# Transformer block on one core: FFN way down in blocks of twelve matmuls instead of triples, `h` moved by 64 bytes, and another order behind the last matmul

## The chip, the cores and the metric

One Trainium2 chip, one of its cores. The metric is the device time in microseconds of one execution of the whole program, all data in HBM at its start and its end.

## The reference

One block of a transformer on 512 tokens of width 1,024, all in float32: a gated FFN, a mixer of two kinds of attention, a second gated FFN, a last RMS norm. Cut to what matters here:

```python
def swiglu(h, w_gate, w_up, w_down):          # 1024 -> 2816 -> 1024
    return (jax.nn.silu(h @ w_gate) * (h @ w_up)) @ w_down

x = x + 0.5 * swiglu(rmsnorm(x, norm_ffn1), w_ffn1_gate, w_ffn1_up, w_ffn1_down)
x = x + hybrid_mixer(rmsnorm(x, norm_mix), ...)
x = x + 0.5 * swiglu(rmsnorm(x, norm_ffn2), w_ffn2_gate, w_ffn2_up, w_ffn2_down)
return rmsnorm(x, norm_final)
```

## The kernel before

Activations stand transposed: eight tiles `x` of 128 features by 512 tokens. Float32 products are made from halves: each operand is split into a rounded part and the rest (`whi`, `wlo` of down weights, `sph`, `spl` of gate and up weights, `h` twice for each hidden tile), and `mm3` (L100) issues three matmuls for one product: high by high, high by low, low by high. The kind of half is `fp32r`.

**The FFN** (class `Ffn`, L192). Hidden features come in 22 tiles `f` of 128, four to a group (`FP`). The first group is computed plainly (`plain`); the others in pairs by a seven-product scheme on blocks (`pair`), whose matmuls have 256 columns and write `pu`, `pv` and `pw`. For each of its steps ScalarE makes `sph`, VectorE `spl` from it, both in six buffers, four steps ahead of TensorE. The hidden tile `h` (tag `h`, pool `hp`) is kept as halves.

**The way down** (`down`, L392) multiplies a group's four hidden tiles with the down weights, for each of eight output tiles `d`: four products of 512 columns into one bank `pd`, so 12 matmuls, and VectorE adds half of the bank to `x` (`half_added`, L531). `mixed` lays the eight steps of one group between the pair steps of the next. In the kernel before, a step doesn't issue its matmuls itself: it puts four triples (`triple`, one `mm3` each) into a list `waiting`, and `run` of the pair steps takes one out with `between` after each of its own products of four, and a second in the middle when more than four wait. `issue_after` holds each triple behind the pair matmul ahead of it. So the 12 matmuls of a `d` stand in four places.

**The end** (from L1108 on). The last two hidden tiles are multiplied the other way round, `h` as weights and `w_down` as the streamed operand, so that the result has tokens on partitions. `turn_x` transposes `x` by TensorE (`px`, 32 of them) into eight tiles `z`. For each of four token tiles `i` and two halves of the width there are six matmuls into `pd`, `residual` adds them to `z` on VectorE (L1130) and sums squares on ScalarE (L1131), and `norm(i)` takes the root on ScalarE (L1135), the reciprocal on VectorE (L1136), scales one half on ScalarE (L1138) and the other on VectorE (L1139), and writes both by SyncE (L1141).

Tiles are placed by pools in the order in which they are asked for, so a tile that nothing reads moves those behind it: `gap` and `rest` are such. In the program before, halves of down weights and `h` both start at byte 32 modulo 256 of a partition; `sph` and `spl` start at byte 96, and what is streamed against them (`xo`, `th`, `tl`) at 32. A scheduler orders each engine's instructions on these dependences.

Of the kernel before, what the change touches and what calls it, by code (L numbers as in the profile page):

```python
# [9 lines left out]
F32 = mybir.dt.float32  # L10
F32R = mybir.dt.float32r
AF = mybir.ActivationFunctionType
# [17 lines left out]
def block_kernel(ctx: ExitStack, tc: tile.TileContext, A: dict, out: bass.AP):  # L30
# [69 lines left out]
    def mm3(p, w, v, first, last, again=False):  # L100
        nc.tensor.matmul(p, w[0], v[0], start=first, stop=False, skip_group_check=again)  # L101
        nc.tensor.matmul(p, w[0], v[1], start=False, stop=False, skip_group_check=again)  # L102
        return nc.tensor.matmul(p, w[1], v[0], start=False, stop=last, skip_group_check=again)  # L103

    def mm2(p, w, v, first, last):

# [21 lines left out]

    gates = cp.tile([128, NT, 24], F32, name="gates")
    pos = cp.tile([128, 2, 32], F32, name="pos")  # L130
    ss = cp.tile([128, 2, NT], F32, name="ss")
# [3 lines left out]
    cp.tile([128, 48], F32, name="rest")  # L135
# [56 lines left out]
    class Ffn:  # L192
# [14 lines left out]
        def __init__(self, wg, wu, which, tmp, hp, sp):  # L207
            self.w, self.which, self.tmp, self.hp, self.sp = (wg, wu), which, tmp, hp, sp
            self.xg, self.hs, self.steps = None, {}, []
            self.b, self.temps = {}, {}  # L210
            self.last_lo = None
            self.x_made = None
            self.waiting = []
            self.in_pair = None
            self.held = 5
# [91 lines left out]
        def pair(self, f):  # L307
# [36 lines left out]
            def copied(m, to, name):  # L344
                part[m, name] = self.sp.tile([128, HT], F32, name="wc", tag="wc", bufs=4)
# [43 lines left out]
                                  lambda m=m, then=then: then(m)])  # L389
            return steps  # L390

        def down(self, w, fs, then, tags=("mm",), groups=(1,) * NK, kept_back=True, left=None):  # L392


            n = len(fs)
            raw, got, bank = {}, {}, {}
# [14 lines left out]
            def run(d):  # L411
                ds = {sum(groups[:g]): range(sum(groups[:g]), sum(groups[:g + 1])) for g in range(len(groups))}.get(d)
                if ds is None:
                    return

                def triple(i, k):
                    if k == 0:
                        bank[i] = pt(tags[i % len(tags)], "pd")
                    with tc.issue_after(self.in_pair.ins) if left != 0 and self.in_pair else nullcontext():
                        mm3(bank[i], got[i, k], self.hs[fs[k]], k == 0, k == n - 1)  # L420
                    if k == n - 1:
                        then(i, bank[i])
# [4 lines left out]
                at = 0 if left is None else len(todo) - (left if ds[-1] == NK - 1 else 0)  # L427
                if at:
                    self.between(len(self.waiting))
                for one in todo[:at]:  # L430
                    one()
                self.waiting += todo[at:]
# [4 lines left out]
        def between(self, n):  # L437

            for _ in range(min(n, len(self.waiting))):
                self.waiting.pop(0)()  # L440

        def mixed(self, steps, fills, tail=1):

# [8 lines left out]
        def lay(self, wd):  # L452

            for f in range(FP):
                self.steps += self.plain(f)
            self.steps += self.down(wd[0], range(FP), half_added, ("s", "t", "o", "mm"), (4, 4), False, 1)
            fills = []
            for f in range(FP, NF, FP):
                fs = range(f, min(f + FP, NF))
                pairs = [step for i in fs[::2] for step in self.pair(i)]  # L460
                self.steps += self.mixed(pairs, fills) if fills else pairs
                if len(fs) == FP:
                    fills = self.down(wd[f // FP], fs, half_added)

        def go(self, after):
# [20 lines left out]
                late = s[4]  # L486
            if late:
                late()
            self.between(len(self.waiting))


    scr_t = dp.tile([16, 128, RVW], F32, name="scr_t")
# [40 lines left out]
    with ExitStack() as ph:  # L533
# [55 lines left out]
            squares(tmp, d, "tmp", 5)  # L589

        ffn.lay(A["wd1a"])
        ffn.steps += ffn.down(A["wd1b"], range(NF - NF % FP, NF), then, (None,), (4, 2, 2), left=0)
        ffn.go(after)


# [495 lines left out]
    with ExitStack() as ph:  # L1091
# [36 lines left out]
        def residual(i, half, p):  # L1128

            nc.vector.scalar_tensor_tensor(z[i, half], p, 0.5, z[i, half], ALU.mult, ALU.add)  # L1130
            nc.scalar.activation(sq, z[i, half], AF.Square, accum_out=ss[:, half, i:i + 1])  # L1131

        def norm(i):
            r = ss[:, 1, i:i + 1]
            nc.scalar.activation(r, r, AF.Sqrt, bias=mean[:, i:i + 1], scale=1.0 / D)  # L1135
            nc.vector.reciprocal(r, r)  # L1136
            y = [xp.tile([128, S], F32, name="xo", tag="xo", bufs=16) for _ in range(2)]
            nc.scalar.activation(y[0], z[i, 0], AF.Copy, scale=r)  # L1138
            nc.vector.scalar_tensor_tensor(y[1], z[i, 1], r, gf[1], ALU.mult, ALU.mult)  # L1139
            for half in range(2):  # L1140
                nc.sync.dma_start(out[i * 128:(i + 1) * 128, half * S:(half + 1) * S], y[half])  # L1141

        last = range(NF - NF % FP, NF)
        w = [load(A["wd2b"][half]) for half in range(2)]
# [2 lines left out]
                z[i, half] = turn_x(i, half)  # L1147
        for i in range(NT):
            b = slice(i * 128, (i + 1) * 128)
            for half in range(2):  # L1150
                p = pt(None, "pd")
                for k, f in enumerate(last):
                    mm3(p, (hs[f][0][:, b], hs[f][1][:, b]), w[half][k], f == last[0], f == last[-1])
                residual(i, half, p)
                if half == 0:
                    nc.gpsimd.tensor_scalar(mean[:, i:i + 1], ss[:, 0, i:i + 1], 1.0 / D, 1e-6, ALU.mult, ALU.add)
                    nc.gpsimd.tensor_tensor(z[i, 0], z[i, 0], gf[0], ALU.mult)
                else:
                    norm(i)


def _buckets(dist):
# [84 lines left out]
```

## Time and profile before

| what | value |
|---|---|
| three runs: median (lowest to highest) | 991.96 us (991.29 to 992.9) |
| the profiled execution | 990.21 us |
| its span, first to last instruction | 988.4 us |
| mean granted TensorE clock, of full speed | 0.997 |
| TensorE busy | 970.5 us, 98% of the span |
| VectorE, ScalarE, GpSimd busy | 778.5, 561.9, 132.5 us |
| first FFN, attention, second FFN with the end | to 351 us, 351 to 634 us, 634 us on |

The profiled execution took 1.8 us more than its span and 1.75 us less than the median. PE is the row of matmuls, PEld that of weight loads, which run beside them. A matmul's record is longer than the distance to the next one's start, since matmuls overlap; where two groups of one shape differ in mean length, their distances differ likewise.

### The profile page before, as it was taken

To read this page: it belongs to the slowest core of one execution; us is meant where nothing else is said; L and a number is where in the kernel's file an instruction comes from. 1 tells how busy PE (TensorE), PEld (TensorE's weight loads), DVE (VectorE), ACT (ScalarE), POOL (GpSimd) and SP (SyncE) were. 2 spreads that over 40 slices of the span, in tenths; PEclk is the share of its full clock that TensorE was granted. 3 is DMA by queue.
4 is the path that set the end of the run, shared out by engine and by line. 5 is a ranking of instruction groups with operands and counts; after the bars stand their busy time and mean duration, and the time that the engine had idled before them with its cause. 6 is when DMAs were issued, how large, how long until landed. Compare 5 with 4: busy or idle time off the path is not lost.

```text
span 988.4 us, 16902 instructions
## 1 busy us (share of the span) xinstructions
PE 970.5 (98%) x6084; PEld 859.0 (87%) x6084; DVE 778.5 (79%) x1579; ACT 561.9 (57%) x1165; POOL 132.5 (13%) x176
## 2 busy tenths in 40 slices
PE   9999999999999999999999999999999999999996
PEld 7789999999999898787878888888999999999985
DVE  6996997688776587768788978789898788777744
ACT  6464655445544366567677886655475445454435
POOL 0000000000000000035666676100000000000002
PEclk9999999999999999999999999999999999999998
DMA  7255534332321125531121232226254322341102
GB/s 257 97 185 173 196 129 133 110 102 91 97 68 43 58 88 190 181 113 33 53 72 43 87 85 80 71 86 213 67 166 153 119 73 95 101 128 44 54 11 86
DMA packets 50056, 104.52 MB, mean 106 GB/s; under 512 B 10129, under 2 KB 14690, under 8 KB 49972
## 3 DMA queue, kind: packets, MB, share of 16 engines
q1 hardware_dynamic: 49684, 102.91, 32.4%
q8 instruction: 48, 0.79, 0.3%
q10 hardware_dynamic: 288, 0.52, 0.1%
q14 instruction: 36, 0.29, 0.1%
HBM read 97.98 MB, written 5.30 MB: 104 GB/s over the span
## 4 chain that ended last, share of the span: by engine, by line
PE 91%; DVE 4%; issue 1%; ACT 1%; DMA 1%; POOL 0%; SPq 0%; POOLq 0%; ACTq 0%; DVEq 0%
PE pd L102 8%; PE pd L103 8%; PE pd L101 8%; PE pu L101 6%; PE pu L103 6%; PE pu L102 6%; PE pw L101 4%; PE pw L103 4%; PE pw L102 4%; PE pp L103 3%; PE pp L101 3%; PE pp L102 3%; PE pgu L102 3%; PE pgu L101 3%; PE pgu L103 3%; PE ps_t L940 3%
## 5 line engine op out<-in xcount | busy, mean ns | idle before, releaser
L236 ACT ACTIVATE sph<-aw 128x512 fp32r<-128x512 f32 x252 | 157.3, 630 | 197.4 <-PE pu L102 71.1
L237 DVE TENSOR_TENSOR spl<-aw,sph 128x512 fp32r<-128x512 f32 x252 | 172.3, 690 | 59.7 <-ACT sph L236 57.2
L92 ACT ACTIVATE whi<-raw 128x512 fp32r<-128x512 f32 (+1 forms) x200 | 121.5, 619 | 126.4 <-PE pd L102 44.2
L102 PE MATMUL pd<-h,whi 128*128 128x512 f32 x336 | 132.7, 395 | 0.0
L103 PE MATMUL pd<-h,wlo 128*128 128x512 f32 x336 | 131.1, 393 | 0.0
L96 DVE TENSOR_TENSOR wlo<-raw,whi 128x512 fp32r<-128x512 f32 (+1 forms) x168 | 111.7, 676 | 24.1 <-ACT whi L92 20.6
L101 PE MATMUL pd<-h,whi 128*128 128x512 f32 x336 | 130.4, 394 | 0.0
L101 PE MATMUL pu<-th,sph 128*128 128x256 f32 x432 | 119.4, 276 | 0.3 <-ACT wc L346 0.3
L103 PE MATMUL pu<-th,spl 128*128 128x256 f32 x432 | 119.4, 276 | 0.0
L102 PE MATMUL pu<-tl,sph 128*128 128x256 f32 x432 | 119.2, 276 | 0.0
L322 DVE TENSOR_TENSOR aw<-aw 128x512 f32<-128x512 f32 x144 | 99.0, 689 | 0.0
L531 DVE SCALAR_TENSOR_TENSOR x<-pd,x 128x512 f32<-128x512 f32 x88 | 60.1, 689 | 33.3 <-PE pd L103 33.3
L101 PEld LDWEIGHTS pu<-th,sph 128*128 128x128 f32 x432 | 81.1, 188 | 4.6 <-ACT wc L346 0.5
L102 PEld LDWEIGHTS pu<-tl,sph 128*128 128x128 f32 x432 | 81.1, 188 | 4.0
L103 PEld LDWEIGHTS pu<-th,spl 128*128 128x128 f32 x432 | 81.1, 188 | 0.1
L101 PE MATMUL pw<-xo,sph 128*128 128x256 f32 x288 | 79.7, 277 | 0.2 <-ACT sph L236 0.2
L102 PE MATMUL pw<-xo,sph 128*128 128x256 f32 x288 | 79.5, 276 | 0.0
L103 PE MATMUL pw<-xo,spl 128*128 128x256 f32 x288 | 79.4, 277 | 0.0
L103 PEld LDWEIGHTS pd<-h,wlo 128*128 128x128 f32 x336 | 63.1, 188 | 13.8
L102 PEld LDWEIGHTS pd<-h,whi 128*128 128x128 f32 x336 | 63.1, 188 | 4.0
L101 PEld LDWEIGHTS pd<-h,whi 128*128 128x128 f32 x336 | 63.1, 188 | 3.7
L101 PEld LDWEIGHTS pw<-xo,sph 128*128 128x128 f32 x288 | 54.1, 188 | 3.9 <-ACT sph L236 0.6
(246 smaller groups left out, 2443.1 us busy)
## 6 DMA issues: line engine op xcount, KB each, us to landing
aw<-in_wg SPq DMA_DIRECT2D x72, 256.0 KB, 2.8
aw<-in_wu SPq DMA_DIRECT2D x72, 256.0 KB, 4.5
raw<-in_wd1a SPq DMA_DIRECT2D x20, 512.0 KB, 3.9
raw<-in_wd2a SPq DMA_DIRECT2D x20, 512.0 KB, 4.8
raw<-in_w_a SPq DMA_DIRECT2D x16, 512.0 KB, 4.8
raw<-in_w SPq DMA_DIRECT2D x8, 512.0 KB, 4.0
raw<-in_w_o SPq DMA_DIRECT2D x8, 512.0 KB, 3.6
raw<-in_wg SPq DMA_DIRECT2D x7, 512.0 KB, 3.6
```

What stands on the lines that cost most here:

```text
L92: last_hi[0] = nc.scalar.activation(hi, v, AF.Copy)
L96: nc.vector.tensor_tensor(lo, v, f32(hi), ALU.subtract)
L101: nc.tensor.matmul(p, w[0], v[0], start=first, stop=False, skip_group_check=again)
L102: nc.tensor.matmul(p, w[0], v[1], start=False, stop=False, skip_group_check=again)
L103: return nc.tensor.matmul(p, w[1], v[0], start=False, stop=last, skip_group_check=again)
L236: nc.scalar.activation(hi, v, AF.Copy)
L237: self.last_lo = nc.vector.tensor_tensor(lo, v, f32(hi), ALU.subtract)
L322: nc.vector.tensor_tensor(to, x, y, op)
L531: nc.vector.scalar_tensor_tensor(xs[d], p, 0.5, xs[d], ALU.mult, ALU.add)
L940: nc.tensor.transpose(p[:, wide:wide + 128], lps[qi][:, j * 128:(j + 1) * 128], ident)
```

## The change

1. `down` loses the list of triples: a step issues its 12 matmuls at once. `between`, `waiting`, `in_pair` and `held` go.
2. Two tiles that nobody reads stand ahead of others: 64 bytes in `hp` ahead of `h`, and 192 bytes in `sp`. `h` starts at byte 96 modulo 256, so that weights' halves minus `h` is 192 where it was 0. All else stays in place modulo 256. With it, `sph` minus `h` (the first weights behind a run of `pd`) is 0 where it was 64, and in the last stage `h` as weights minus the streamed `w_down` is 64 where it was 0.
3. The last token tile's second half is computed in two pieces of 256 columns. `norm(i - 1)` is called behind tile `i`, its reciprocal behind the last addition to `z`, its `xo` behind a small addition; one of the last two output DMAs is issued by ScalarE.

```diff
+            hp.tile([128, 16], F32, name="gap_h", tag="gap_h", bufs=1)
+            sp.tile([128, 48], F32, name="gap_t", tag="gap_t", bufs=1)
...
-                    self.in_pair = mm3(bank[m, to], (hi[:, k], lo[:, k]), x, first and k == 0, k == 3, not first)
-                    if k == 1:
-                        self.between(self.held == 0 and len(self.waiting) > 4)
-                self.between(self.held == 0)
-                self.held = max(self.held - 1, 0)
+                    mm3(bank[m, to], (hi[:, k], lo[:, k]), x, first and k == 0, k == 3, not first)
...
-                todo = []
+                for i in ds:
+                    bank[i] = pt(tag, "pd")
                 for ks in ([range(n)] if len(ds) == 1 else [range(n - 1), range(n - 1, n)]):
-                    todo += [lambda i=i, k=k: triple(i, k) for i in ds for k in ks]
...
+                    for i in ds:
+                        for k in ks:
+                            mm3(bank[i], got[i, k], self.hs[fs[k]], k == 0, k == n - 1)
+                for i in ds:
+                    then(i, bank[i])
...
-        def norm(i):
-            r = ss[:, 1, i:i + 1]
+        def norm(i, part):
+            r = ss[:, part, i:i + 1]
             nc.scalar.activation(r, r, AF.Sqrt, bias=mean[:, i:i + 1], scale=1.0 / D)
-            nc.vector.reciprocal(r, r)
+            with tc.issue_after(added[0].ins):
+                nc.vector.reciprocal(r, r)
...
+                queue = nc.scalar if i == NT - 1 and half == 0 else nc.sync
+                queue.dma_start(out[i * 128:(i + 1) * 128, half * S:(half + 1) * S], y[half])
...
-            for half in range(2):
-                p = pt(None, "pd")
+            parts = [slice(0, S), slice(0, S)] if i < NT - 1 else [slice(0, S), slice(0, S // 2), slice(S // 2, S)]
+            for part, cols in enumerate(parts):
+                p = pt(None, "pd")[:, cols]
...
+                elif part < len(parts) - 1:
+                    summed_up[0] = nc.vector.scalar_tensor_tensor(
+                        mean[:, i:i + 1], ss[:, 1, i:i + 1], 1.0 / D, mean[:, i:i + 1], ALU.mult, ALU.add)
+            if i:
+                norm(i - 1, 1)
+        norm(NT - 1, 2)
```

What it does to the order. TensorE in the second FFN, before, at one triple (the numbers tell buffers apart):

```order
L103 MATMUL pu_10454<-xo_8272,spl_10385 128x256
L101 MATMUL pd_10434<-h_9673,whi_10337 128x512
L102 MATMUL pd_10434<-h_9674,whi_10337 128x512
L103 MATMUL pd_10434<-h_9673,wlo_10338 128x512
L102 MATMUL pv_10508<-xo_8255,sph_10414 128x256
```

and now, at one block:

```order
L103 MATMUL pu_10500<-th3_7814,spl_10558 128x256
L101 MATMUL pd_10674<-h_10035,whi_10582 128x512
L102 MATMUL pd_10674<-h_10036,whi_10582 128x512
L103 MATMUL pd_10674<-h_10035,wlo_10583 128x512
L101 MATMUL pd_10674<-h_10107,whi_10582 128x512
L102 MATMUL pd_10674<-h_10108,whi_10582 128x512
L103 MATMUL pd_10674<-h_10107,wlo_10583 128x512
L101 MATMUL pd_10674<-h_10413,whi_10582 128x512
L102 MATMUL pd_10674<-h_10414,whi_10582 128x512
L103 MATMUL pd_10674<-h_10413,wlo_10583 128x512
L101 MATMUL pd_10674<-h_10459,whi_10582 128x512
```

The block ends with two more and goes on with `pw`. Over the whole program before, 230 runs of `pd` have three matmuls; now 66 runs that follow on other matmuls have eight or more (51 of them twelve), and 17 have one to four. Both hold the same 1,008 matmuls on `h`. The order of attention is the same in both.

VectorE's last rows, before (`z` from `pd` is the addition of a half, `xo` an output):

```order
L1130 SCALAR_TENSOR_TENSOR z<-pd,z 128x512 x2
L1136 RECIPROCAL ss<-ss 128x1
L1130 SCALAR_TENSOR_TENSOR z<-pd,z 128x512
L1139 SCALAR_TENSOR_TENSOR xo<-z,ss,gf 128x512
L1136 RECIPROCAL ss<-ss 128x1
L1139 SCALAR_TENSOR_TENSOR xo<-z,ss,gf 128x512
```

and now:

```order
L1110 SCALAR_TENSOR_TENSOR z<-pd,z 128x512
L1110 SCALAR_TENSOR_TENSOR z<-pd,z 128x256 x2
L1117 RECIPROCAL ss<-ss 128x1
L1144 SCALAR_TENSOR_TENSOR mean<-ss,mean 128x1
L1121 SCALAR_TENSOR_TENSOR xo<-z,ss,gf 128x512
L1117 RECIPROCAL ss<-ss 128x1
L1121 SCALAR_TENSOR_TENSOR xo<-z,ss,gf 128x512
```

The third tile's reciprocal no longer stands ahead of the last addition, and that addition has 256 columns. ScalarE's last rows, before (`sqd` sums squares):

```order
L1131 ACTIVATE sqd,ss<-z 128x512
L1138 ACTIVATE xo<-z,ss 128x512
L1131 ACTIVATE sqd,ss<-z 128x512
L1135 ACTIVATE ss<-ss,mean 128x1
L1138 ACTIVATE xo<-z,ss 128x512
```

and now:

```order
L1111 ACTIVATE sqd,ss<-z 128x512
L1111 ACTIVATE sqd,ss<-z 128x256 x2
L1119 ACTIVATE xo<-z,ss 128x512
L1115 ACTIVATE ss<-ss,mean 128x1
L1119 ACTIVATE xo<-z,ss 128x512
L1124 DMA out<-xo 128x512
```

The third tile's `xo` has moved behind the last sum of squares and ahead of the last root. On TensorE the 32 transposes of `turn_x`, which before stood in five places between `pd` matmuls, now stand in one row ahead of the last stage.

## Rows read from the trace of the kernel before

**Rows 1.** The page, part 1 (busy time, share of the span, instructions of each engine) and part 4 (the chain that ended last, share of the span by engine).

```profile
PE 970.5 (98%) x6084; PEld 859.0 (87%) x6084; DVE 778.5 (79%) x1579; ACT 561.9 (57%) x1165; POOL 132.5 (13%) x176
...
PE 91%; DVE 4%; issue 1%; ACT 1%; DMA 1%; POOL 0%; SPq 0%; POOLq 0%; ACTq 0%; DVEq 0%
```

**Rows 2.** The windows view, the stretch of the second FFN in which its triples lie. Columns: stretch, its length, then busy us (and instructions) of PE, PEld, DVE, ACT, POOL, the granted clock, DMA share, GB/s.

```profile
710.00:940.00 230.00, 229.78 (x1692) 215.45 (x1691) 185.21 (x326) 120.49 (x236) 0.00 (x0) 1.00 0.33 106
```

**Rows 3.** The timeline, PE alone, around one triple: the last `pu` ahead of it, its first matmul, and the first matmul behind it. Columns: start us, us of the matmul, engine, line, operation, out<-in, tile, count.

```profile
251.13 0.28 PE L103 MATMUL pu<-th,spl 128*128 128x256 f32 x1
251.24 0.40 PE L101 MATMUL pd<-h,whi 128*128 128x512 f32 x1
...
251.94 0.28 PE L101 MATMUL pw<-xo,sph 128*128 128x256 f32 x1
```

**Rows 4.** The groups by line and form, PE alone, of the stretch 150 to 290 us, where every `pd` stands in a triple. Columns: busy us, mean ns of one, idle time before.

```profile
L102 PE MATMUL pd<-h,whi 128*128 128x512 f32 x73 | 29.0, 397 | 0.0
L101 PE MATMUL pd<-h,whi 128*128 128x512 f32 x73 | 28.8, 395 | 0.0
L103 PE MATMUL pd<-h,wlo 128*128 128x512 f32 x73 | 28.8, 394 | 0.0
```

**Rows 5.** The same view of the stretch 333.2 to 350.8 us, inside the one run of 84 `pd` matmuls at the end of the first FFN (the other two lines also have 389).

```profile
L102 PE MATMUL pd<-h,whi 128*128 128x512 f32 x26 | 10.1, 389 | 0.0
```

**Rows 6.** The timeline, PE alone: the 1st, the 7th and the 84th matmul of that run.

```profile
331.78 0.40 PE L101 MATMUL pd<-h,whi 128*128 128x512 f32 x1
...
333.16 0.39 PE L101 MATMUL pd<-h,whi 128*128 128x512 f32 x1
...
350.62 0.39 PE L103 MATMUL pd<-h,wlo 128*128 128x512 f32 x1
```

**Rows 7.** The groups by line and form, PE alone, of 331.95 to 333.15 us: the first six matmuls of that run.

```profile
L101 PE MATMUL pd<-h,whi 128*128 128x512 f32 x2 | 0.8, 395 | 0.0
L102 PE MATMUL pd<-h,whi 128*128 128x512 f32 x2 | 0.8, 395 | 0.0
L103 PE MATMUL pd<-h,wlo 128*128 128x512 f32 x2 | 0.8, 389 | 0.0
```

**Rows 8.** The page, part 5: all FFN down matmuls whose weights are `whi`, `wlo` and whose streamed operand is `h`.

```profile
L102 PE MATMUL pd<-h,whi 128*128 128x512 f32 x336 | 132.7, 395 | 0.0
L103 PE MATMUL pd<-h,wlo 128*128 128x512 f32 x336 | 131.1, 393 | 0.0
L101 PE MATMUL pd<-h,whi 128*128 128x512 f32 x336 | 130.4, 394 | 0.0
```

**Rows 9.** The groups by line and form, PE alone, of the whole span: one of the gate and up matmuls, one of another stage with 256 columns, and the dearest group of 32 with 512 columns.

```profile
L101 PE MATMUL pu<-th,sph 128*128 128x256 f32 x432 | 119.4, 276 | 0.3 <-ACT wc L346 0.3
L749 PE MATMUL pc<-whi,ak 128*128 128x256 f32 x32 | 8.0, 284 | 0.0
L101 PE MATMUL pw<-o,whi 128*128 128x512 f32 x32 | 13.0, 405 | 0.0
```

**Rows 10.** The waits of 100 to 350 us: us in total, times, longest us.

```profile
DVE spl L237 <- ACT sph L236: 24.9, 36, 1.5
ACT whi L92 <- PE pd L102: 24.2, 17, 3.7
```

**Rows 11.** The waits of PE alone, 40 to 400 us, both rows.

```profile
PE pu L101 <- ACT wc L346: 0.3, 1, 0.3
PE pw L101 <- ACT sph L236: 0.2, 1, 0.2
```

**Rows 12.** The timeline, PE alone, eight transposes between down matmuls in the last stage, and the matmul behind them.

```profile
960.07 1.03 PE L1116 MATMUL px<-ident,x 128*128 128x128 f32 x8
960.86 0.48 PE L101 MATMUL pd<-h,whi 128*128 128x512 f32 x1
```

**Rows 13.** The timeline of all engines from the last matmul to the last instruction that computes; in brackets the idle time before a row and what ended it.

```profile
979.84 0.39 PE L103 MATMUL pd<-whi,h 128*128 128x512 f32 x1
...
981.18 0.16 DVE L1136 RECIPROCAL ss<-ss 128x1 f32<-128x1 f32 x1 [0.64 <-ACT ss L1135]
981.26 0.67 DVE L1130 SCALAR_TENSOR_TENSOR z<-pd,z 128x512 f32<-128x512 f32 x1
981.67 0.71 ACT L1138 ACTIVATE xo<-z,ss 128x512 f32<-128x512 f32 x1
...
982.28 0.61 ACT L1131 ACTIVATE sqd<-z 128x512 f32<-128x512 f32 x1
983.08 0.29 ACT L1135 ACTIVATE ss<-ss,mean 128x1 f32<-128x1 f32 x1
983.40 0.16 DVE L1136 RECIPROCAL ss<-ss 128x1 f32<-128x1 f32 x1 [0.81 <-ACT ss L1135]
...
983.75 0.72 ACT L1138 ACTIVATE xo<-z,ss 128x512 f32<-128x512 f32 x1 [0.37 <-POOL z L1157]
```

**Rows 14.** The groups by line: the nearest rows of DVE and ACT on half as many columns (of 150 to 290 us).

```profile
L362 DVE TENSOR_TENSOR t<-pu,wc 128x256 f32<-128x256 f32 x10 | 4.2, 425 | 8.6 <-PE pu L103 8.6
L346 ACT ACTIVATE wc<-pu 128x256 f32<-128x256 f32 x18 | 6.6, 367 | 0.0
```

**Rows 15.** The view of line L1141, the eight DMAs that write the output.

```profile
L1141 SPq DMA_DIRECT2D out<-xo x8: 332/344/384, 977.2 to 984.9; - x8
DMA to landing us min/median/max: 2.1/2.3/2.6
```

More of the change, by code (lines that the diff above doesn't have):

```diff
@@ L102, in mm3 @@
         nc.tensor.matmul(p, w[0], v[1], start=False, stop=False, skip_group_check=again)
-        return nc.tensor.matmul(p, w[1], v[0], start=False, stop=last, skip_group_check=again)
+        nc.tensor.matmul(p, w[1], v[0], start=False, stop=last, skip_group_check=again)
     def mm2(p, w, v, first, last):
@@ L130, in block_kernel @@
     pos = cp.tile([128, 2, 32], F32, name="pos")
-    ss = cp.tile([128, 2, NT], F32, name="ss")
+    ss = cp.tile([128, 3, NT], F32, name="ss")
     mean = cp.tile([128, NT], F32, name="mean")
@@ L134, in block_kernel @@
     far = cp.tile([32, 16], F32, name="far")
-    cp.tile([128, 48], F32, name="rest")
+    cp.tile([128, 40], F32, name="rest")
     ones_f = cp.tile([128, 128], F32, name="ones_f")
@@ L390, in pair, with down @@
             return steps
-        def down(self, w, fs, then, tags=("mm",), groups=(1,) * NK, kept_back=True, left=None):
+        def down(self, w, fs, then, tag="mm", groups=(1,) * NK, kept_back=True):
             n = len(fs)
@@ L455, in lay @@
                 self.steps += self.plain(f)
-            self.steps += self.down(wd[0], range(FP), half_added, ("s", "t", "o", "mm"), (4, 4), False, 1)
+            self.steps += self.down(wd[0], range(FP), half_added, None, (4, 4), False)
             fills = []
@@ L488, in go @@
                 late()
-            self.between(len(self.waiting))
     scr_t = dp.tile([16, 128, RVW], F32, name="scr_t")
@@ L591, in block_kernel @@
         ffn.lay(A["wd1a"])
-        ffn.steps += ffn.down(A["wd1b"], range(NF - NF % FP, NF), then, (None,), (4, 2, 2), left=0)
+        ffn.steps += ffn.down(A["wd1b"], range(NF - NF % FP, NF), then, None, (4, 2, 2))
         ffn.go(after)
@@ L1126, in block_kernel, with residual @@
         z = {}
-        def residual(i, half, p):
-            nc.vector.scalar_tensor_tensor(z[i, half], p, 0.5, z[i, half], ALU.mult, ALU.add)
-            nc.scalar.activation(sq, z[i, half], AF.Square, accum_out=ss[:, half, i:i + 1])
-        def norm(i):
-            r = ss[:, 1, i:i + 1]
+        summed_up = [None]
+        def residual(i, part, p, cols):
+            v = z[i, min(part, 1)][:, cols]
+            added[0] = nc.vector.scalar_tensor_tensor(v, p, 0.5, v, ALU.mult, ALU.add)
+            nc.scalar.activation(sq[:, cols], v, AF.Square, accum_out=ss[:, part, i:i + 1])
+        def norm(i, part):
+            r = ss[:, part, i:i + 1]
             nc.scalar.activation(r, r, AF.Sqrt, bias=mean[:, i:i + 1], scale=1.0 / D)
-            nc.vector.reciprocal(r, r)
+            with tc.issue_after(added[0].ins):
+                nc.vector.reciprocal(r, r)
             y = [xp.tile([128, S], F32, name="xo", tag="xo", bufs=16) for _ in range(2)]
             nc.scalar.activation(y[0], z[i, 0], AF.Copy, scale=r)
-            nc.vector.scalar_tensor_tensor(y[1], z[i, 1], r, gf[1], ALU.mult, ALU.mult)
+            with tc.issue_after(summed_up[0].ins) if summed_up[0] else nullcontext():
+                nc.vector.scalar_tensor_tensor(y[1], z[i, 1], r, gf[1], ALU.mult, ALU.mult)
             for half in range(2):
-                nc.sync.dma_start(out[i * 128:(i + 1) * 128, half * S:(half + 1) * S], y[half])
+                queue = nc.scalar if i == NT - 1 and half == 0 else nc.sync
+                queue.dma_start(out[i * 128:(i + 1) * 128, half * S:(half + 1) * S], y[half])
         last = range(NF - NF % FP, NF)
@@ L1149, in block_kernel @@
             b = slice(i * 128, (i + 1) * 128)
-            for half in range(2):
-                p = pt(None, "pd")
+            parts = [slice(0, S), slice(0, S)] if i < NT - 1 else [slice(0, S), slice(0, S // 2), slice(S // 2, S)]
+            for part, cols in enumerate(parts):
+                p = pt(None, "pd")[:, cols]
                 for k, f in enumerate(last):
-                    mm3(p, (hs[f][0][:, b], hs[f][1][:, b]), w[half][k], f == last[0], f == last[-1])
-                residual(i, half, p)
-                if half == 0:
+                    mm3(p, (hs[f][0][:, b], hs[f][1][:, b]), [v[:, cols] for v in w[min(part, 1)][k]],
+                        f == last[0], f == last[-1])
+                residual(i, part, p, cols)
+                if part == 0:
                     nc.gpsimd.tensor_scalar(mean[:, i:i + 1], ss[:, 0, i:i + 1], 1.0 / D, 1e-6, ALU.mult, ALU.add)
                     nc.gpsimd.tensor_tensor(z[i, 0], z[i, 0], gf[0], ALU.mult)
-                else:
-                    norm(i)
+                elif part < len(parts) - 1:
[4 more added lines that the diff above has]
+        norm(NT - 1, 2)
 def _buckets(dist):
```

19 lines of the change are left out of this document (removed).

## The prediction, made before the changed kernel ran

> **What bounds the kernel now.** I read the page first: TensorE is busy for 98% of the span and makes 91% of the chain that ended last [rows 1]. So I look for time in what TensorE's matmuls cost and in the end, where it has stopped. The windows of the second FFN's triples say the same more sharply: 229.78 of 230.00 us busy at full granted clock, VectorE 185 and ScalarE 120 [rows 2]. TensorE's own waits from 40 to 400 us come to 0.5 us [rows 11]. Nothing is to be won in the FFNs by freeing another engine; there the change can only act through the distance from one matmul to the next.
>
> That distance isn't the same everywhere. Inside the long run of `pd` the 7th to the 84th matmul start 17.46 us apart [rows 6], 226.8 ns each, and last 389 ns by the record [rows 5]. In triples the records have 397, 395 and 394 [rows 4]: 8 + 6 + 5 = 19 ns more for three. The starts agree: 251.24 to 251.94 is 0.70 us [rows 3], three settled distances are 0.68. The run of 84 pays as well, but once, at its head: its first six records are 395, 395 and 389 in pairs [rows 7], 24 ns in all, and 333.16 - 331.78 = 1.38 us [rows 6] against 1.36. So a run of `pd` that follows on 256-column matmuls pays about 19 ns when it has three and 24 ns when it is long, then nothing.
>
> **The change part by part.** *Blocks.* All 1,008 matmuls on `h` together stand above 389 by 336 x (6 + 4 + 5) ns = 5.0 us [rows 8]. In the new order 66 runs are long: 66 x 24 = 1.6 us; 17 short ones pay at most 19 each, 0.3 us. So 5.0 becomes 1.9: **-3.1 us**, all on TensorE's path, if a block pays what a run pays today.
>
> *The new place of `h`.* No run of 512-column matmuls at a distance of 192 stands in the trace, so this is bounded. From below: nothing is paid at the heads, 1.9 us better than above. A floor under 389 isn't excluded either: at 256 columns the `pc` matmuls (weights and stream both at byte 32) have 284 and the `pu` matmuls (64 apart) 276 [rows 9], so distance may be worth 8 ns a matmul, or 8.1 us over 1,008. From above: every `pd` is as dear as the dearest of a triple, 397, which is 8.1 us over the floor where 5.0 are paid now, so 3.1 us worse than before; or as the dearest group of 512 columns, 405 [rows 9], 16.1 us, 11.1 worse. I take the head's price as it is, 24 ns, since the row nearest to a block of twelve is the run of 84 of the same tiles, and it lies between. Where `sph` follows on a block it is 0 from `h` instead of 64; `pu` then `pd` at 0 already runs at 276 in the mean. 48 matmuls of the last stage get 64 instead of 0: at 8 ns either way 0.4 us, counted as nothing.
>
> [...] Equal shapes take 389 here and 397 there, with TensorE always busy. [...]
>
> *What else the blocks move.* VectorE adds a bank after every block as it did after every fourth triple, some 0.7 us either way. A `whi` buffer comes free when a whole block is through; ScalarE, which waits in order, already stood 24.2 us for such (17 times), and VectorE 24.9 us for `sph` [rows 10], while TensorE lost 0.5 us [rows 11]. The four steps whose halves are made ahead are the cover; I cost this at nothing. If the cover is gone, `spl` is late next and TensorE stands.
>
> *Transposes in one row.* The matmul behind a group of `px` lasts 0.48 us instead of 0.39 [rows 12]. Of five such groups one is left: 4 x 0.09 = 0.36, of which two are already in the 5.0 us above. **-0.2 us**, ends 0 and -0.4. The last `px` need the last addition to `x`; 25 others stand ahead of them, at 0.79 us for eight [rows 12] some 2.5 us, against 0.7 for the addition.
>
> *The end.* Before, the last matmul starts at 979.84; VectorE could add at about 980.25, but stands behind the third tile's reciprocal, which waits for a root, and adds at 981.26. ScalarE's last `xo` ends at 983.75 + 0.72 = 984.47 [rows 13]. Now the last addition has 256 columns (0.43 by the nearest row, sum of squares 0.37 [rows 14]): 980.25 + 0.43, sum from 980.7; root about 0.56 later instead of the 0.80 of before (983.08 - 982.28), 981.26, but the third tile's `xo` stands ahead of it in ScalarE's line, +0.71, 981.97; from root to last `xo` 0.67 (983.75 - 983.08), 982.64, and its 0.72: 983.36. That is 1.1 less. The two last output DMAs are issued by two engines, which saves one issue of 0.34 us, but both still move 256 KB and land 2.1 to 2.6 us later [rows 15], so I count none. **-1.1 us**; ends 0 (ScalarE comes late to its last row, as it did before) and -2.1 (the third tile's `xo` fits into a gap, and the issue counts).
>
> Sum: -3.1 - 0.2 - 1.1 = -4.4 us. The profiled execution took 990.21 us for a span of 988.4, 1.75 us below the median of the runs; the sum of its own is 985.8. Taken from the median of 991.96 it is **987.6 us**.
>
> **The rivals.** *A: distance 192 runs better than 0.* Every `pd` falls below today's floor, by the 8 ns that parts `pc` from `pu` [rows 9]: -5.0 - 8.1 - 1.3 = -14.4, **977.6 us**. For it: the 256-column rows differ by distance. Against it: the settled 389 [rows 5] is the shortest mean of this shape that I found, and `pd` ahead of `sph`, 64 apart, is no shorter (394, the third of a triple [rows 4]). [...]
>
> *B: distance 192 is a bad one.* In every matmul on `h` the stream and the next weight load disturb each other throughout, not just at the head. Price: 405 as in the dearest group [rows 9], +11.1 - 1.3 = +9.8, **1001.8 us**. It turns into a loss where the mean record on `h` is above 389 by more than (5.0 + 1.3) / 1,008 = 6.3 ns, and one beyond 0.2% from 8.2 ns on. For it: disturbance at distance 0 exists in triples. Against: at 0 and at 64 it dies out or never comes.
>
> *C: blocks starve the pairs.* ScalarE waits for a block's `whi` and makes `sph` late; the wait becomes TensorE's. TensorE's waits of this kind are 0.2 to 0.3 us [rows 11]; at 0.25 in one of three of the 66 blocks it is 5.5 us, which leaves +1.1: **993.1 us**. For it: ScalarE's long waits [rows 10]. Against: VectorE and ScalarE have 45 and 110 us to spare in 230 [rows 2].
>
> *D: the place of `h` does nothing and the end gives nothing* (ScalarE is late): -3.3, 988.7 us, inside the forecast's own range.
>
> **How the numbers follow.** Chances: the forecast with D 0.66, A 0.10, B 0.09, C 0.15. The forecast's own range is 985 to 990. Two parts in a hundred, 0.2% or 2.0 us, are about what a measurement here tells from no change. Faster by more than that (below 990.0): forecast and A, and a little of C, 0.77; within it: most of C and the mild part of B, 0.14; slower (above 993.9): the rest of B and C, 0.09. The range of 8 in 10 leaves out A's far end and B, and takes in half of C: 982.0 to 992.5.
>
> **What would show it.** Right: mean records on `h` of 389 to 391, with one dear head in a run of twelve; windows of the second FFN with PE busy throughout; the last `z` starting within 0.1 us of TensorE's end; last matmul to last `xo` about 3.5 us instead of 4.63. Wrong: records on `h` above 395 in the middle of blocks (B) or below 385 (A); TensorE waiting for `sph`, `wc` or `wlo` by several us (C); a last `xo` that waits for ScalarE's line (the end's term).

## The result and the profile after

The change makes the kernel slower, by 0.7%: 998.32 us median (997.55 to 999.62, 6 runs) against 991.55 us (990.36 to 992.9, 6 runs), a ratio of 1.0067 with an interval of 1.0057 to 1.0078. The forecast was 987.6 us in a range of 982.0 to 992.5, with 0.09 for slower; it was wrong. The profiled execution took 999.62 us for a span of 997.8, 1.3 us over its median; that of before, 990.21 us, was 1.3 us under.

TensorE is as busy as before (98% of the span [rows 1]); it waits 1.7 us in the FFNs (0.9 at `pgu`, 0.8 at `pu`), 1.3 us before. The groups that answer to [rows 8] and to the first of [rows 9], from the groups of the changed kernel's lines (busy us, mean ns of one, idle time before):

```profile
L102 PE MATMUL pd<-h,whi 128*128 128x512 f32 x336 | 132.1, 393 | 0.0
L103 PE MATMUL pd<-h,wlo 128*128 128x512 f32 x336 | 131.3, 392 | 0.0
L101 PE MATMUL pd<-h,whi 128*128 128x512 f32 x336 | 129.6, 393 | 0.0
L101 PE MATMUL pu<-th,sph 128*128 128x256 f32 x432 | 120.9, 280 | 0.2 <-ACT wc L341 0.2
L103 PE MATMUL pu<-th,spl 128*128 128x256 f32 x432 | 120.8, 280 | 0.0
L102 PE MATMUL pu<-tl,sph 128*128 128x256 f32 x432 | 120.8, 280 | 0.0
```

The matmuls on `h`, of which the prediction speaks, are a little cheaper: 394.2 us in all before, 393.0 now. What lost is what nobody touched: the 256-column matmuls of the pairs went from 276 to 280 ns. These three groups grow by 4.5 us, the groups of `pu` and `pv` from `xo` and of `pw`, of the same shape, by 4.0 more (pw 80.4, 80.3 and 79.5 us against 79.7, 79.5 and 79.4). One stretch of the first FFN shows it in starts (timeline of TensorE in the changed kernel; start, duration):

```profile
203.21 0.28 PE L101 MATMUL pu<-th,sph 128*128 128x256 f32 x1
...
205.92 0.28 PE L103 MATMUL pu<-th,spl 128*128 128x256 f32 x1
206.04 0.40 PE L101 MATMUL pd<-h,whi 128*128 128x512 f32 x1
...
208.81 0.28 PE L101 MATMUL pv<-xo,sph 128*128 128x256 f32 x1
```

24 matmuls from 203.21 to 206.04 are 117.9 ns each, with no gap in which TensorE waits for anything. In the kernel before, such a stretch runs at 113.3. The block of twelve lasts 2.77 us, 47 ns more than twelve times the 226.7 ns at which starts settle in a long run.

The two spans differ by 9.4 us: +8.5 from the 256-column matmuls, -1.2 from those on `h`, +0.3 at the end, -0.5 at the start and +2.0 in the attention stage, which the change doesn't touch, make 9.1 of them. That last part is TensorE's granted clock (windows; PE busy with its count, PEld, DVE, ACT, POOL, clock, DMA share, GB/s):

```profile
405.00:411.00 6.00, 4.98 (x25) 4.40 (x26) 4.44 (x12) 3.34 (x9) 0.00 (x0) 0.72 0.59 169
466.00:469.00 3.00, 3.00 (x11) 2.07 (x9) 2.33 (x8) 2.44 (x8) 0.45 (x1) 0.50 0.01 3
```

It is 0.50 in the second stretch and falls to that for a part of the first; before it is 1.00 in both. From 403 to 407 us, ahead of the first fall, TensorE was busy for 2.57 of 4.00 us, and from 460 to 466 us for 4.28 of 6.00; in the same work before it was 2.58 (400 to 404 us) and 4.31, so these rows don't tell what brought it down. Of the kernels below, with the same attention, tail_act's profile has such a fall (285.3 us for the stage) and that of blocks_h0 hasn't (283.6): it can come without the blocks and stay away with them. Without it the difference is 7.4 us, near the 6.8 of the medians.

**The trace of before had this.** In the first FFN its pairs begin among longer runs of `pd`. This is what follows on one (timeline of TensorE in the kernel before; the run that ends with the matmul at 80.99 has 17 of them):

```profile
80.99 0.39 PE L103 MATMUL pd<-h,wlo 128*128 128x512 f32 x1
81.22 0.28 PE L103 MATMUL pu<-xo,spl 128*128 128x256 f32 x1
...
85.69 0.28 PE L103 MATMUL pw<-xo,spl 128*128 128x256 f32 x1
85.81 0.40 PE L101 MATMUL pd<-h,whi 128*128 128x512 f32 x1
...
86.28 0.39 PE L103 MATMUL pd<-h,wlo 128*128 128x512 f32 x1
86.51 0.28 PE L102 MATMUL pu<-tl,sph 128*128 128x256 f32 x1
...
90.93 0.28 PE L101 MATMUL pu<-th,sph 128*128 128x256 f32 x1
```

39 matmuls from 81.22 to 85.81 run at 117.7 ns; then comes a triple; the next 39, from 86.51 to 90.93, run at 113.3. The triple that looks dear by its own records puts the stream behind it right.

### The profile page after: what moved, and what is told of

Its sections match the earlier page's. It is cut to its first block, busy times and chain, and to the rows that moved or that the text cites. A ratio compares the mean times of both kernels' runs of the same rounds, so it can differ in the third digit from the quotient of the medians.

```text
span 997.8 us, 16928 instructions
## 1 busy us (share of the span) xinstructions
PE 979.6 (98%) x6090; PEld 870.1 (87%) x6090; DVE 782.8 (78%) x1581; ACT 566.1 (57%) x1167; POOL 133.1 (13%) x176
## 4 chain that ended last, share of the span: by engine, by line
PE 93%; DVE 3%; DMA 1%; issue 1%; ACT 1%; SPq 0%; DVEq 0%; ACTq 0%
PE pd L103 8%; PE pd L101 8%; PE pd L102 8%; PE pu L101 7%; PE pu L103 7%; PE pu L102 7%; PE pw L101 5%; PE pw L103 5%; PE pw L102 5%; PE pp L103 3%; PE pp L101 3%; PE pp L102 3%; PE pgu L101 3%; PE pgu L102 3%; PE pgu L103 3%; PE pv L101 3%
## 5 line engine op out<-in xcount | busy, mean ns | idle before, releaser
L101 PE MATMUL pw<-xo,sph 128*128 128x256 f32 x288 | 80.4, 280 | 0.0
L102 PE MATMUL pw<-xo,sph 128*128 128x256 f32 x288 | 80.3, 279 | 0.0
L103 PE MATMUL pw<-xo,spl 128*128 128x256 f32 x288 | 79.5, 279 | 0.0
L102 PEld LDWEIGHTS pd<-h,whi 128*128 128x128 f32 x336 | 63.2, 188 | 11.1
```

## The experiments

The theories, as the texts on record name them. **T**: the 256-column stream has two lasting rates, and blocks at distance 192 that the order breaks put it into the slow one. **R1**: the distance does it. **R2**: the blocks do it at any distance. Later **T2**: at distance 0 a run of up to three `pd` matmuls leaves the stream fast, one of four or more slow; against **R4**: it is the block and what hangs on it. "Distance" with 0 or 192 is one of addresses, in bytes, as in the prediction; times in ns are from one matmul's start to the next. A stream of 256-column matmuls is called fast at 113.3 ns and slow at 117.8. A line of the form 276/276/285 is the least, the median and the largest duration in ns of a group of instructions on the tile `pu` between 200 and 290 us.

**blocks_h0: the change without its address.**

```diff
-            hp.tile([128, 16], F32, name="gap_h", tag="gap_h", bufs=1)
-            sp.tile([128, 48], F32, name="gap_t", tag="gap_t", bufs=1)
```

> The change without its new address: blocks of 12, the order of TensorE's instructions and the end as changed, but h at byte 32 modulo 256 again, distance 0. Theory T (256-column matmuls run at one of two rates, 113 or 118 ns apart, and runs of pd at distance 192 leave them in the slow one): the records of pu stand at 276 ns as before, pd at 392 or less, time 987 to 990 us against 991.5 before. Rival R1 (distance 192 by itself makes whatever follows slow): the same numbers. Rival R2 (blocks of 12 do it at any distance): pu at 280 ns, 996 to 998 us.

Measured: 997.77 us against 991.78, ratio 1.0061 (1.0047 to 1.0075).

```profile
L101 PE MATMUL pu<-th,sph x72: 281/281/282, 202.5 to 289.4; 128*128 128x256 f32 x72
```

T fell here, and R1 as the cause of the loss: at distance 0 the same blocks lose as much. R2 had both numbers. The groups on `h` come to 131.6 + 130.5 + 129.3 = 391.4 us, 2.8 less than before, which is the prediction's term of 3.1 nearly whole; the stream behind takes it back four times over (the groups of the 256-column matmuls grow by 11.1 us).

**triples_h192: the address alone.** The two lines of above, put into the kernel before.

> The change's address alone: triples, their order and the end as before, h moved by 64 bytes, distance 192. R1: pu at 280 ns, the 2,900 matmuls of 256 columns lose some 4 ns each beside dear triples, 1000 us or more. R2: pu at 276, pd near 393, 991 to 992 us. T: the rate depends on the length of the run, and no run of 3 at distance 192 is in the trace except in the middle of blocks that the order breaks, where the matmuls behind it were fast; so 276 and 991 to 992 us is the likelier, 280 and 1000 is possible.

Measured: 995.68 us, ratio 1.0033 (1.0020 to 1.0045); TensorE's timeline:

```profile
203.16 0.39 PE L101 MATMUL pd<-h,whi 128*128 128x512 f32 x1
...
203.85 0.28 PE L101 MATMUL pu<-th,sph 128*128 128x256 f32 x1
...
204.56 0.28 PE L101 MATMUL pu<-th,sph 128*128 128x256 f32 x1
...
205.24 0.39 PE L101 MATMUL pd<-h,whi 128*128 128x512 f32 x1
```

The triple costs less (0.69 us, 7 to 8 ns over three settled distances instead of 20), but the six matmuls behind it take 0.71 us, the six after these 0.68: 27 ns more. So the address costs some 15 ns a triple, 3.4 us for 230, by itself. None of the three theories had this time: T and R2 said 991 to 992 us, R1 1000 or more.

**whole_h192: the changed kernel with its blocks whole** (one in each FFN still falls into 7 and 5).

```diff
+                    with tc.issue_after(self.last_pd.ins) if self.last_pd else nullcontext():
-                    mm3(bank[m, to], (hi[:, k], lo[:, k]), x, first and k == 0, k == 3, not first)
+                        self.in_pair = mm3(bank[m, to], (hi[:, k], lo[:, k]), x, first and k == 0, k == 3, not first)
...
+                            with tc.issue_after(self.in_pair.ins) if self.in_pair else nullcontext():
-                            mm3(bank[i], got[i, k], self.hs[fs[k]], k == 0, k == n - 1)
+                                self.last_pd = mm3(bank[i], got[i, k], self.hs[fs[k]], k == 0, k == n - 1)
```

> The changed kernel at distance 192, but with the first blocks of each FFN kept whole: they no longer fall apart into runs of 1, 3, 4, 2 and 10 ahead of the runs of 12. T: nothing puts the 256-column matmuls into the slow rate, and runs of 12 keep the rate that they find: pu at 276 and 113 ns, 988 to 990 us. R1 and R2 (the run of 12 or the distance makes them slow, however they began): pu at 280, 996 to 998 us.

Measured: 994.58 us, ratio 1.0020 (1.0012 to 1.0029).

```profile
L101 PE MATMUL pu<-th,sph x72: 276/276/285, 203.6 to 285.5; 128*128 128x256 f32 x72
```

Half of T is right. At distance 192 the outcome depends on the stream ahead of the block: a block that comes on a fast one costs 27 ns and leaves five slow matmuls, then a fast stream (in 58 of 59), one that comes on a slow one costs 46 or 47 and leaves it slow (42 of 42 in the changed kernel). The time stayed 5 us above T's: besides the five, the second FFN has 372 matmuls at 117.8 behind its first long run, with no run in between to end the slow rate, the first FFN has a part of such a stretch, and TensorE waits 1.4 us for `wlo`.

**quads_h0: runs of 4 in place of 3, distance 0.** The list of waiting steps holds single `pd` matmuls, and a counter of the pairs' `mm3` calls releases them:

```diff
-                    if k == 1:
-                        self.between(self.held == 0 and len(self.waiting) > 4)
-                self.between(self.held == 0)
+                    self.slot()
...
-                    todo += [lambda i=i, k=k: triple(i, k) for i in ds for k in ks]
+                    todo += [lambda i=i, k=k, j=j: one_of(i, k, j) for i in ds for k in ks for j in range(3)]
...
+            n, gap = [(4, 5), (4, 5), (4, 6)][self.turn % 3]
+            self.credit += 1
+            if self.credit >= (gap if len(self.waiting) <= 15 else min(gap, 3)) and len(self.waiting) >= n:
+                ...
+                self.between(n)
```

> The kernel before, with its address (distance 0) and its end, but the pd matmuls between the pairs' matmuls come in runs of 4 instead of 3, a run each 15 or 18 matmuls of 256 columns instead of each 12. Theory T2, formed on the traces so far (at distance 0 a run of up to 3 leaves the 256-column stream behind it at 113.3 ns, a run of 4 or more at 117.8): pu goes from 276 to 280, some 2,300 to 2,900 matmuls lose 4.5 ns each, +10 to +13 us, the runs' heads win 1 us: 1000 to 1003 us against 991.6. Rival R4 (it is the block, a whole bank's 12 matmuls with their buffers, or the 512-column time per stretch, not the step from 3 to 4): pu stays at 276, 990 to 992 us.

Measured: 1003.22 us against 991.47, ratio 1.0115 (1.0099 to 1.0131).

```profile
L101 PE MATMUL pu<-th,sph x71: 281/281/281, 201.7 to 290.0; 128*128 128x256 f32 x71
```

As T2 said, and the sharpest of the tests: one matmul more in each run, no block, no other buffers, and the whole stream changes its rate. (What differs besides: the runs stand 15 or 18 matmuls apart instead of 12, and the pairs' matmuls are bound to come behind the run ahead of them.)

**singles_h0: each `pd` matmul alone.** The same list with `[(1, 1)]`.

> The kernel before, its address and its end, but each pd matmul between the pairs stands alone, one behind every three matmuls of 256 columns, 650 of them in place of 230 triples. T2: the stream stays at 113.3 (pu 276), and a lone pd costs about 4 ns over 226.7 (the three in the trace of the blocks at distance 0: 231), 650 x 4 = 2.6 us in place of 230 x 20 = 4.6 us: 989.5 to 990 us against 991.6. Rival (each pd pays the dear first distance of a triple, 6 ns, and each return to 256 columns pays another 5): 650 x 11 = 7.2 us, 994 us.

Measured: 1003.13 us, ratio 1.0113 (1.0096 to 1.0129). T2's number was wrong by 13 us, the rival's by 9 (timeline of TensorE):

```profile
164.94 0.40 PE L420 MATMUL pd<-h,whi 128*128 128x512 f32 x1
165.17 0.28 PE L101 MATMUL pw<-xo,sph 128*128 128x256 f32 x1
165.30 0.28 PE L102 MATMUL pw<-xo,sph 128*128 128x256 f32 x1
165.41 0.28 PE L103 MATMUL pw<-xo,spl 128*128 128x256 f32 x1
165.53 0.40 PE L420 MATMUL pd<-h,whi 128*128 128x512 f32 x1
```

On a fast stream a lone `pd` takes 235 ns, and the three behind it 121, 116 and 114: 8 + 11 = some 20 ns. A triple costs 20 ns as well, so a lone `pd` pays there what three together pay. The 4 ns that I had carried over were of lone matmuls on a slow stream. This price holds for the first FFN alone. In the second one, TensorE waits 0.5 us for `t` at 753 us, the stream comes out of it slow, and no lone `pd` behind it makes it fast (timeline of TensorE):

```profile
764.17 0.39 PE L420 MATMUL pd<-h,wlo 128*128 128x512 f32 x1
764.40 0.28 PE L101 MATMUL pu<-th,sph 128*128 128x256 f32 x1
...
766.17 0.40 PE L420 MATMUL pd<-h,whi 128*128 128x512 f32 x1
```

The 15 matmuls from 764.40 to 766.17 are 118 ns each, and so are those in all 14 places behind 753 us where that many follow on a lone `pd`; each of these comes three matmuls behind another. T2 said that the stream stays fast, so its rule isn't whole. By the starts, the 256-column matmuls cost 9.1 us more here than before and `pd` the same. The profiled spans differ by 14.6 us, of which 1.9 are a fall of the granted clock in attention; the other 3.6 haven't been traced.

**flip_h0: 11, three matmuls of 256 columns, 1.** The same list with `[(11, 15), (1, 1)]`; each `mm3` of a pair and each `pd` is issued after the one before.

> Blocks at distance 0 whose last matmul is taken off: 11 pd matmuls, 3 matmuls of 256 columns, 1 pd matmul, then some 45 matmuls of 256 columns; the end as before. T2: the 11 leave the stream at 117.8, the lone one sets it back to 113.3; a block costs 26 + 3 x 4.5 + 4 = 44 ns where four triples cost 80; 62 of them save 2.2 us: pu at 276 to 277, 989 to 990 us against 991.6, 7 to 8 below the same blocks whole. Rivals R2 and R4 (a block of this size makes what follows slow whatever comes behind): pu at 280, 996 to 998 us.

Measured: 1010.38 us, ratio 1.0186 (1.0164 to 1.0208). The rates came as T2 said (`pu` 276 to 277), the time didn't, for a reason of its own (waits of TensorE: us, times, longest):

```profile
PE pu L101 <- ACT t L368: 9.1, 4, 2.6
PE pd L420 <- DVE h L270: 5.2, 2, 2.7
PE pu L101 <- DVE t L371: 1.5, 2, 1.0
```

The order bound from the start makes TensorE stand 15.8 us ahead of 125 us in the first FFN and at the same place of the second, where the scheduler before had put other matmuls in between. In the second FFN the granted clock falls to about a half behind three of these waits, for 13.7 us in all (windows; 0.51 in one of the three):

```profile
763.00:768.20 5.20, 5.20 (x27) 5.20 (x27) 5.20 (x10) 1.35 (x4) 0.00 (x0) 0.51 0.00 0
```

From 755 to 760 us, before this fall, TensorE was busy for 2.81 of 5.00 us. Matmuls of 256 columns start 213 ns apart in such a stretch, those of 512 columns 427 (as in the changed kernel from 408 to 411 us, where its clock is 0.50); that is some 5.8 us more in the three. The waits, 14.5 us more than before, and this come to 20.3 us; the profiled spans differ by 20.2.

**whole24_h0 and flip24_h0: runs of 24, and of 23 with one set apart.** The order is bound from the first such run only.

```diff
-            n, gap = (24, 32) if self.turn else (3, 1)
+            n, gap = [(23, 31), (1, 1)][(self.turn + 1) % 2] if self.turn else (3, 1)
```

> The same with the lone pd matmul put back into its run: runs of 24, nothing behind them, 30 runs. T2: each leaves the stream at 117.8 ns, some 2,000 matmuls of 256 columns lose 4.5 ns, +9 us, the heads win 3.8: pu at 279 to 280, 996 to 998 us, 8 to 9 above the kernel with the lone matmul. Rival R4 (not the run's end but how much pd comes at once sets the rate): the same time and the same pu as with the lone matmul set apart.

> The kernel before with its address (distance 0) and its end; between the pairs 23 pd matmuls in a run, then 3 matmuls of 256 columns, 1 pd matmul, then some 93 matmuls of 256 columns; the order of the first pairs, ahead of the first such run, is left free as before, so that TensorE shouldn't stand there for t and h as in the blocks of 11 and 1. T2: 30 runs at 26 + 3 x 4.5 + 4 = 44 ns, 1.3 us in place of the 4.6 us of 230 triples: pu at 276 to 277, 987.8 to 988.8 us against 991.5. Rival (blocks cost more than they give, whatever the stream's rate: TensorE waits for halves, banks and h as the prediction's rival C has it): pu at 276 but 992 us or more.

Measured: 997.11 us for the runs of 24 (ratio 1.0046, 1.0034 to 1.0059) and 994.15 with the one set apart (1.0019, 1.0010 to 1.0028), both against 992.42. The same group of `pu`, first of whole24_h0, then of flip24_h0:

```profile
L101 PE MATMUL pu<-th,sph x76: 281/281/281, 201.0 to 288.8; 128*128 128x256 f32 x76
```

```profile
L101 PE MATMUL pu<-th,sph x76: 276/276/281, 202.1 to 287.9; 128*128 128x256 f32 x76
```

One matmul of 24, moved behind three others, sets the rate of the next 93 (in 30 of 30 places): R4 fell. The time of the second kernel is T2's rival's all the same, since its long blocks make TensorE wait (4.2 us for `t` of VectorE, in four places): here the prediction's rival C exists, at blocks of 24.

**flip12_h0: the blocks of 11 and 1 with the first pairs' order left free.**

```diff
+            n, gap = [(11, 15), (1, 1)][(self.turn + 1) % 2] if self.turn else (3, 1)
```

> The blocks of 11 and 1 once more, with the order of the first pairs left free, so that TensorE doesn't stand 15 us for t and h there. T2: 60 blocks at 44 ns, 2.6 us in place of 4.6: pu at 276 to 277, 989 to 990 us. Rival (the 16 us above the expectation in the run with the order bound from the start came from the blocks): 1005 us or more.

Measured: 989.18 us against 992.42, ratio 0.9968 (0.9959 to 0.9977): this beats both kernels, the one before by 0.3%. The timeline of TensorE, one block's end and the next one's head:

```profile
199.94 0.28 PE L101 MATMUL pu<-th,sph 128*128 128x256 f32 x1
...
200.18 0.28 PE L103 MATMUL pu<-th,spl 128*128 128x256 f32 x1
200.30 0.39 PE L421 MATMUL pd<-h,wlo 128*128 128x512 f32 x1
200.53 0.28 PE L101 MATMUL pu<-th,sph 128*128 128x256 f32 x1
...
205.63 0.63 PE L421 MATMUL pd<-h,whi 128*128 128x512 f32 x2
```

Behind the eleven, 118 ns each; then the lone `pd`, 231 ns; then 45 matmuls in 5.10 us, 113.3 each. By the starts a `pd` takes 228.8 ns in the mean, 231.6 before: 2.8 us less for 1,008. The 256-column ones take 114.25 in the mean and 113.88 before, 1.1 us more for 3,024. That is 1.7 us of the 3.2 between the medians; the profiled spans differ by 1.1 (987.3 against 988.4), so the size of the gain is known less well than its sign.

The lengths of the runs at distance 0 that stand between 256-column matmuls, with the mean time from start to start of the next eight, or of fewer where the next run comes sooner (below 115.2 or above 116.2 ns):

| kernel | runs that leave the stream at 113.3 | at 117.8 |
|---|---|---|
| before | 2 of 2, 230 of 3 | 2 each of 6, 10 and 17 |
| blocks_h0 | 3 of 1, 6 of 2, 3 of 3 | 5 of 4, 4 of 8, 6 of 10, 50 of 12, 2 each of 16 and 20 |
| quads_h0 | none | 170 of 4, 2 of 7 |
| whole24_h0 | 2 each of 2 and 3 | 30 of 24, 2 each of 10 and 17 |
| flip24_h0 | 30 of 1, 2 each of 2 and 3 | 30 of 23, 2 each of 10 and 17 |
| singles_h0 (runs with eight or more behind) | 16 of 1, in the first FFN or at the start of the second | 14 of 1, behind 753 us; 2 of 7 |
| flip12_h0 | 60 of 1, 2 each of 2 and 3 | 58 of 11, 2 each of 4, 7, 10 and 17 |

Runs of two and three, and of four and more, have no exception here. A lone `pd` has: it makes a slow stream fast behind blocks, but not in the second FFN of singles_h0.

Behind a wait of TensorE the rate can change too. No run was made to test this; the traces show it (timeline of TensorE in the kernel before):

```profile
743.38 0.28 PE L102 MATMUL pv<-xo,sph 128*128 128x256 f32 x1
743.88 0.39 PE L101 MATMUL pu<-xo,sph 128*128 128x256 f32 x1 [0.22 <-ACT t L368]
744.10 0.28 PE L102 MATMUL pu<-xo,sph 128*128 128x256 f32 x1
...
745.99 0.28 PE L103 MATMUL pv<-xo,spl 128*128 128x256 f32 x1
```

Up to 743.38 the stream is fast; the 16 matmuls from 744.10 to 745.99 are 118 ns each, and it stays so until the next triple. In blocks_h0 a matmul at the same place that starts 0.36 us after the one before it, at 748.07, turns a slow stream fast, and in tail_only a wait of 0.42 us there leaves a fast one fast.

**tail_only: the changed end in the kernel before.**

```diff
-            for half in range(2):
-                p = pt(None, "pd")
+            parts = [slice(0, S), slice(0, S)] if i < NT - 1 else [slice(0, S), slice(0, S // 2), slice(S // 2, S)]
...
+                    summed_up[0] = nc.vector.scalar_tensor_tensor(
+                        mean[:, i:i + 1], ss[:, 1, i:i + 1], 1.0 / D, mean[:, i:i + 1], ALU.mult, ALU.add)
```

> The kernel before with the changed end alone (the last tile's second half in two parts of 256 columns, VectorE's order, two queues for the last rows). The prediction's term: last matmul to last xo 3.5 us instead of 4.63, 990.4 us against 991.5. Rival, from the trace of the changed kernel, where this took 4.70 us since the addition for the root's bias took 0.99 us on VectorE beside GpSimd's multiplication by gf: 4.7 us here too, 991.4 to 991.9 us.

Measured: 991.60 us against 991.78, ratio 1.0003 (0.9993 to 1.0013): nothing that the runs can tell. From the last matmul to the last `xo` it takes 4.54 us in the profile, 4.63 before. The changed kernel's own end (timeline; the releaser in brackets):

```profile
990.77 1.26 POOL L1142 TENSOR_TENSOR z<-z,gf 128x512 f32<-128x512 f32 x1
991.06 0.99 DVE L1144 SCALAR_TENSOR_TENSOR mean<-ss,mean 128x1 f32<-128x1 f32 x1 [0.67 <-ACT sqd L1111]
991.26 0.71 ACT L1119 ACTIVATE xo<-z,ss 128x512 f32<-128x512 f32 x1
992.15 0.29 ACT L1115 ACTIVATE ss<-ss,mean 128x1 f32<-128x1 f32 x1 [0.18 <-DVE mean L1144]
992.88 0.72 ACT L1119 ACTIVATE xo<-z,ss 128x512 f32<-128x512 f32 x1 [0.44 <-DVE ss L1117]
```

An addition of one column takes 0.99 us and ends with GpSimd's multiplication, at 992.05 and 992.03; ScalarE's root waits for it. In the profile of tail_only the two end at 982.84 and 982.83, and the addition again takes 0.99. That GpSimd's work makes it long is my guess from these ends; no run shows it.

**tail_act: that addition on ScalarE.**

```diff
-                    summed_up[0] = nc.vector.scalar_tensor_tensor(
-                        mean[:, i:i + 1], ss[:, 1, i:i + 1], 1.0 / D, mean[:, i:i + 1], ALU.mult, ALU.add)
+                    nc.scalar.activation(mean[:, i:i + 1], ss[:, 1, i:i + 1], AF.Identity, bias=mean[:, i:i + 1],
+                                         scale=1.0 / D)
```

> The kernel before with the changed end, in which the small addition for the root's bias (128x1, 0.99 us on VectorE in the changed kernel, while GpSimd multiplies z by gf) is made on ScalarE. If the two engines' sharing made it long: about 0.2 us on ScalarE, the root 0.7 to 0.9 us earlier, last matmul to last xo 3.7 to 4.0 us instead of 4.7, 990.7 to 991.0 us. Rival (the end waits for ScalarE's line anyway, which holds the third tile's root and xo): 4.5 to 4.8 us, 991.5 us as with VectorE's addition.

Measured: 991.42 us against 991.47, ratio 0.9997 (0.9986 to 1.0008).

```profile
984.16 0.40 ACT L1133 ACTIVATE sqd<-z 128x256 f32<-128x256 f32 x1
984.55 0.70 ACT L1141 ACTIVATE xo<-z,ss 128x512 f32<-128x512 f32 x1
985.17 0.28 ACT L1166 ACTIVATE mean<-ss,mean 128x1 f32<-128x1 f32 x1
985.48 0.29 ACT L1137 ACTIVATE ss<-ss,mean 128x1 f32<-128x1 f32 x1
986.06 0.72 ACT L1141 ACTIVATE xo<-z,ss 128x512 f32<-128x512 f32 x1 [0.29 <-DVE ss L1139]
```

The addition takes 0.28, and the rival is right in the main: ScalarE now has no gap from the last sum of squares to the root, with the third tile's `xo` in front of it. From the last matmul to the last `xo` it takes 4.44 us, a little less than the rival's 4.5 to 4.8. The program ends no earlier than the runs can tell.

## Why the prediction was wrong, by its steps

**Blocks, -3.1 us.** Right as far as it went. At distance 0 the groups on `h` lose 2.8 us, and a block pays 26 ns at its head where the forecast had 24. At distance 192 in the slow stream it is 46 to 47, which leaves 1.2, and the mean records on `h` stand at 392 to 393 where 389 to 391 was to show it right.

**The step that failed** is the premise of the first part: that a run's price is what stands in the run. The prediction compared the triples of `pd` with the run of 84 and saw 19 ns that the triple wastes. It didn't read the 256-column matmuls behind the one and the other. A triple's 20 ns buy a fast stream, at 113.3 ns; a run of four or more saves per matmul and leaves 4.5 ns on each of the 256-column matmuls up to the next short run. With 48 of these between two blocks, at distance 0 four triples cost 80 ns, one block 26 + 48 x 4.5 = 242. In the changed kernel 42 blocks come on a slow stream and leave it slow: 42 x 48 x 4.5 ns = 9.1 us, where the groups of these matmuls grew by 8.5. The prediction has no such term.

**The place of `h`, no change.** As a sum it held, by luck, since two effects cancel: with blocks the two addresses give the same time (1.0067 and 1.0061, intervals overlapping), but at 0 `pd` gains 2.8 us and the 256-column matmuls lose 11.1, at 192 it is 1.2 and 8.5. Alone, on triples, the address costs 0.33%, again not in `pd` (which is cheaper) but behind it. Rival B had a time near the measured one, 1001.8, for a reason that isn't there: no matmul on `h` came near 405 in its mean. That the stream and a weight load disturb each other was a supposition, which no run shows.

**`pu` then `pd` "already runs at 276 in the mean".** The same step fails here: the sentence takes 276 from the row as if it belonged to the shape, and it was the mean of a stream that triples kept fast.

**The end, -1.1 us.** It gave nothing: 4.70 us from the last matmul to the last `xo`, where the forecast had 3.5. The root stood behind VectorE's small addition, 0.99 us, which the working had not counted; and with that away ScalarE's line is the bound, which was the term's lower end.

**Rival C** didn't come in this change (1.7 us of waits, 1.3 before); it came where I bound the order (15.8 us) and at blocks of 24 (4.2 us).

**Transposes, -0.2 us**: not tried by themselves.

A slip that changes no number: "two parts in a hundred" stands beside 0.2%, which is two in a thousand.

What stays open is why. The traces show two rates and, for runs of two or more, what switches them. They don't show what in TensorE holds a rate through hundreds of matmuls, nor when a wait or a lone `pd` changes it.

## What to carry over

Where two shapes of matmul alternate on a saturated TensorE, cost a reordering by the start distances of both shapes, behind each kind of run that the trace has, not by the dear records inside the runs. Look for a long and a short run in the trace of before and read what follows on each. When an order helps only if it is bound, bind it from the place where it matters: the same blocks took 1010.4 us bound from the start and 989.2 bound later.

## What was not expected of the hardware

In these traces the start distance of one and the same matmul (128x128 weights, 256 columns, full granted clock, no wait) settles at 113.3 or at 117.8 ns and keeps its value through hundreds of matmuls: 229 in a row from 713.14 to 739.00 us in the changed kernel, 113.4 in the mean, and 372 at 117.8 in whole_h192. At distance 0 a run of two or three 512-column matmuls leaves it at 113.3 (before: 232 of 232) and one of four or more at 117.8 (quads_h0: 172 of 172); behind some waits of TensorE it changes as well, in either direction (to 117.8 behind 0.22 us in the kernel before, to 113.3 behind a start 0.36 us after the last in blocks_h0). At distance 192 between weights and stream the switch works otherwise than at 0: in whole_h192 a block of twelve on a fast stream leaves five slow matmuls in 58 of 59 places (118, 117, 117, 123, 118 ns, then 113), in the changed kernel one on a slow stream leaves it slow in 42 of 42.
